# Handing over between stages of a decoder layer: when low weights, sums and the first input tile are made

## The chip, the cores and the metric

The kernel runs on one core of one Trainium2 chip. The metric is the time of one execution in device microseconds (us). Of the kernel before, three runs were timed: 2383.11, 2387.39 and 2387.43, median 2387.39.

## The reference: what is computed

One inference step of a decoder layer, for 256 tokens of a prompt and 8 single tokens of running requests (264 together), of width 2048, in float32:

```python
h = h + 0.5 * rmsnorm(swiglu(rmsnorm(h, ffn1_pre), ...), ffn1_post)     # FFN1
h = h + rmsnorm(mix(rmsnorm(h, mix_pre)), mix_post)                     # mixer
h = h + 0.5 * rmsnorm(swiglu(rmsnorm(h, ffn2_pre), ...), ffn2_post)     # FFN2
gate = sigmoid(rmsnorm(h, ple_pre) @ w_ple_gate)
h = h + rmsnorm(gate * (p @ w_ple_proj), ple_post)                      # PLE
```

`rmsnorm(x, g)` is `x * rsqrt(mean(x*x) + 1e-6) * g`, the mean over the 2048 channels of a token. `swiglu` is `(silu(x @ wg) * (x @ wu)) @ wd` with an inner width of 5632. `mix` projects its input, runs a gated convolution and a state-space scan (48 heads) side by side, and projects both back (the out-projection). The outputs are the layer's result and the new states of the convolutions and the scan.

## The kernel before

**Tiles.** Activations lie feature-major: a tile is 128 channels by 264 tokens, so a 2048-channel tensor is 16 tiles (KD = 16). `H(k)` is tile k of h, four to a buffer. A product with a weight matrix goes column by column: a column is 128 outputs, the sum over all k tiles of 128 x 128 weights in one bank of PSUM.

**Three matmuls for one.** Each float32 is split into a high part rounded for TensorE and a low part, the rest. `mm3` issues high weight by high input (L277), high weight by low input (L278) and low weight by high input (L279). For inputs `split` lets ScalarE write the high half (L268, `act<-h,vec`) and VectorE the low half (L244, `act<-h,vec,act`). For weights `Weights.load` brings a unit of 14 or 16 tiles by DMA from SyncE in two pieces of up to eight (L170), casts each to its high part on ScalarE (L172, `whi`) and subtracts on VectorE (L175, `wlo`). Of the buffers `wraw`, `whi` and `wlo` there are four each, and units are loaded two ahead of the one in use, so a cast starts when TensorE has read the last tile of an older piece.

**Stages.** FFN1, mixer, FFN2 and PLE follow each other with no gap but their norms. FFN1, FFN2 and PLE begin with a first pass (`gemm_first`): seven columns at a time over k = 0 to 15, unit by unit with two k tiles each, seven accumulators (two of them in the small banks `ps`). Then the rest goes column by column (`gemm_one`), for the FFNs in three chunks of the inner width with a down projection behind each (`ys`). The out-projection makes its columns in pairs (`gemm_pair`).

**Norms.** `SumSq.add` squares a tile on ScalarE and adds it to a running tile `run` (on GpSimd, for a first pass on VectorE); the last `direct` squares stay apart. `total` (L339) multiplies the parts by a matrix of ones, which sums over the channels and leaves the result on all partitions; one such matmul in float32 is two records of TensorE. `rsqrt` is a logarithm and an exponential on ScalarE. A first pass doesn't wait for its own norm, as the input isn't scaled by it: the scale is applied to the columns behind it. There `late` issues the total behind k tile 14 (of 0 to 15) as the scheduler finds room, and `eq` (L421, on VectorE) is made from it, a term that keeps the epsilon of the norm; the bank of the total is reused by the eighth column, which therefore waits until `eq` is read from it.

**A handover** is what lies between a stage's last column and the next stage's first matmul: the last addition to y (L241), its square (L268), the total, the scale `rs` (L268 twice), for the first tile the residual (`tmp<-y,vec,rr` at L244 and the addition to h at L241), its high and low halves, then the first matmul. TensorE does warm matmuls meanwhile (`warm`, L379), `HANDOVER = (4, 11)` of them ahead of the last part of the total and behind it; each is two records. `update_input` issues the handover's residuals and splits for tiles 0 to 3 in program order, the others as the scheduler places them.

**The order.** A scheduler with a model of the engines' times fixes one queue for each engine ahead of the run, and each engine works off its queue in that order. `high_priority`, `issue_after` and `keep_in_program_order` steer it.

**The tail.** `esq.total` gives the last norm. Then y = h + e*r is made tile by tile: on GpSimd for tiles 12 to 15, on VectorE by multiply and add, or, for the tiles in `TAIL_TENSOR`, by VectorE's multiply, two matmuls with the identity into PSUM (L1188 for h, L1220 for e) and a copy by ScalarE (L1221). Each finished tile or pair of tiles is stored (`store`, L1206).

## Time and profile before

| | us |
|---|---|
| median of three runs | 2387.39 |
| lowest and highest run | 2383.11, 2387.43 |
| the profiled execution's own time | 2383.33 |
| its span, first to last instruction | 2381.6 |
| mean granted clock of TensorE (1 is full speed) | 0.999 |
| low weights on VectorE (L175), busy | 978.1 |
| casts of weights on ScalarE (L172), busy | 831.4 |

The two last rows are from the page's groups, 814 instructions each. In a row of the timeline stand the start, the length, the engine, the line, the operation, the output and inputs, and in brackets how long the engine was idle before it and what ended that. Lengths of instructions that follow each other overlap a little; the distance of their starts is what one costs. For TensorE the ends are modelled, so distances of starts are used throughout. Names are shortened: `act` is a split input, `tmp` a temporary, `rr` a tile with a scale, `acc` and `ps` are banks of PSUM.

### The profile page before, as it was taken

How to read it: one execution, taken by the hardware profiler on the slowest of the kernel's cores; microseconds unless marked ns; L12 is line 12 of the kernel's file. 1: busy time of each engine (PE TensorE's matmuls, PEld its weight loads, DVE VectorE, ACT ScalarE, POOL GpSimd, SP SyncE). 2: the span in 40 equal slices, each digit the busy share in tenths (PEclk: the TensorE clock that was granted, in tenths of full speed). 3: DMA queues.
4: the chain of work that ended last, by engine and by line, in shares of the span. 5: the costliest groups of instructions: out<-in, count | busy, mean ns of one | idle time of the engine just before them, and what ended most of it. 6: DMA issues, size and time to landing. Idle time of an engine off the chain costs nothing.

```text
span 2381.6 us, 47454 instructions
## 1 busy us (share of the span) xinstructions
PE 2361.7 (99%) x19534; PEld 2342.3 (98%) x19534; DVE 1576.5 (66%) x2382; ACT 1186.8 (50%) x1787; POOL 178.0 (7%) x201
## 2 busy tenths in 40 slices
...
GB/s 260 217 184 182 184 184 182 185 184 182 184 173 183 257 229 230 215 222 211 224 214 180 180 168 236 163 232 244 227 211 228 238 241 212 221 234 207 179 206 134
DMA packets 163434, 489.89 MB, mean 206 GB/s; under 512 B 25312, under 2 KB 43024, under 8 KB 163216
## 3 DMA queue, kind: packets, MB, share of 16 engines
...
q14 instruction: 65, 0.53, 0.1%
...
## 4 chain that ended last, share of the span: by engine, by line
PE 94%; DVE 2%; ACT 2%; issue 1%; DMA 1%; SPq 0%; POOL 0%; ACTq 0%; DVEq 0%; POOLq 0%
PE acc L277 30%; PE acc L278 30%; PE acc L279 30%; PE ps L277 1%; PE ps L278 1%; PE ps L279 1%; DVE wlo L175 1%; ACT whi L172 1%; PE ps L339 1%; PE ps L906 1%; DMA wraw<-in_w 0%; PE ps L891 0%; DVE h L241 0%; DMA d_bc<-rows 0%; DVE ych L851 0%
## 5 line engine op out<-in xcount | busy, mean ns | idle before, releaser
L279 PE MATMUL acc<-act,wlo 128*128 128x264 f32 x6128 | 1733.0, 285 | 1.9 <-DVE wlo L175 1.9
L278 PE MATMUL acc<-act,whi 128*128 128x264 f32 x6128 | 1719.9, 282 | 0.0
L277 PE MATMUL acc<-act,whi 128*128 128x264 f32 x6128 | 1703.7, 282 | 2.5 <-ACT whi L172 2.2
L175 DVE TENSOR_TENSOR wlo<-wraw,whi 128x1024 fp32r<-128x1024 f32 (+2 forms) x814 | 978.1, 1204 | 584.9 <-ACT whi L172 581.3
L172 ACT CAST whi<-wraw 128x1024 fp32r<-128x1024 f32 (+2 forms) x814 | 831.4, 1024 | 974.2 <-PE acc L278 682.8
L277 PEld LDWEIGHTS acc<-act,whi 128*128 128x128 f32 x6128 | 1147.5, 189 | 5.1 <-ACT whi L172 2.9
L279 PEld LDWEIGHTS acc<-act,wlo 128*128 128x128 f32 x6128 | 1144.7, 187 | 5.5 <-DVE wlo L175 3.5
L278 PEld LDWEIGHTS acc<-act,whi 128*128 128x128 f32 x6128 | 1146.8, 187 | 1.9 <-issue 0.9
L241 POOL TENSOR_TENSOR run<-run,tmp 128x264 f32<-128x264 f32 x77 | 72.2, 938 | 889.6 <-ACT tmp L268 889.2
L244 DVE SCALAR_TENSOR_TENSOR y<-v,vec,y 128x245 f32<-128x245 f32 (+23 forms) x240 | 106.2, 465 | 0.6
L241 POOL TENSOR_TENSOR s<-s,eap 128x1024 f32<-128x1024 f32 x24 | 47.0, 1960 | 629.6 <-DMA s<-in_hst 534.4
L244 DVE SCALAR_TENSOR_TENSOR s<-bb,xds,s 128x128 f32<-128x128 f32 x192 | 52.7, 346 | 60.0 <-POOL s L241 60.0
L241 DVE TENSOR_TENSOR tmp<-acc,rr 128x264 f32<-128x264 f32 x99 | 42.5, 430 | 50.2 <-PE acc L279 50.2
L286 ACT CAST act<-tmp 128x264 fp32r<-128x264 f32 x104 | 41.9, 411 | 55.6 <-DVE tmp L241 50.9
L241 DVE TENSOR_TENSOR tmp<-tmp,acc 128x264 f32<-128x264 f32 x84 | 35.9, 428 | 39.9 <-PE acc L279 39.4
L241 DVE TENSOR_TENSOR act<-tmp,act 128x264 fp32r<-128x264 f32 x120 | 52.4, 441 | 0.5 <-ACT act L286 0.5
L278 PE MATMUL ps<-act,whi 128*128 128x264 f32 x192 | 52.3, 283 | 0.0
L279 PE MATMUL ps<-act,wlo 128*128 128x264 f32 x192 | 52.1, 284 | 0.0
L268 ACT ACTIVATE tmp<-tmp 128x264 f32<-128x264 f32 x112 | 47.0, 420 | 6.9 <-DVE tmp L241 6.7
L268 ACT ACTIVATE tmp<-y 128x264 f32<-128x264 f32 x67 | 28.0, 425 | 44.7 <-DVE y L241 43.3
L241 POOL TENSOR_TENSOR run<-run,y 128x264 f32<-128x264 f32 x7 | 7.2, 1029 | 576.7 <-ACT run L321 499.2
L241 DVE TENSOR_TENSOR y<-y,acc 128x264 f32<-128x264 f32 x80 | 34.0, 425 | 23.8 <-PE acc L279 23.8
(170 smaller groups left out, 1038.9 us busy)
## 6 DMA issues: line engine op xcount, KB each, us to landing
...
```

Of the source, the lines that this page charges most:

```text
L172: self.hi = nc.scalar.copy(hi[:, c:d], raw[:, c:d]).ins
L175: nc.vector.tensor_tensor(out=lo[:, c:d], in0=raw[:, c:d], in1=hi[:, c:d].bitcast(F32), op=ALU.subtract)
L241: return (eng or nc.vector).tensor_tensor(out=out, in0=in0, in1=in1, op=op)
L244: return nc.vector.scalar_tensor_tensor(out=out, in0=in0, scalar=scalar, in1=in1, op0=op0, op1=op1)
L268: i = nc.scalar.activation(out=out, in_=in_, func=func, bias=bias, scale=scale)
L277: nc.tensor.matmul(acc, hi, x[:, 0, :], start=first, stop=False)
L278: nc.tensor.matmul(acc, hi, x[:, 1, :], start=False, stop=False)
L279: traced[0] = nc.tensor.matmul(acc, lo, x[:, 0, :], start=False, stop=last).ins
L286: nc.scalar.copy(t[:, 0, :], x)
L339: m = nc.tensor.matmul(p, ones, s, start=i == 0, stop=last)
L906: nc.tensor.matmul(pd[64 * q : 64 * q + 64, P * c : P * c + P], xdt[c][:, 2 * j + q, :], ab[c][:, 2 * j + q, :], start=True, stop=True,)
```

## The change

1. *Low weights later at the two handovers.* For the unit loaded at the last pair of the out-projection, and for the one at the last down column of FFN2, `Weights.load(defer="second")` leaves both subtractions and the second cast for later. `flush` issues the first subtraction behind the last addition to y, the second cast and subtraction behind the last square.
2. *First input tile direct.* `update_input` no longer waits for the residual in h for tile 0. With the product of both gains (`both`, made once on GpSimd) VectorE forms t = y0 * both * rs, writes H(0) * pre + t once rounded, as the high half, and once in full, and subtracts for the low half. H(0)'s residual follows behind tile 3's. All squares of the new input go into `run`, so its total is one matmul and not two.
3. *The total in first passes.* `late` is now issued ahead of the fourth column of the last k tile, 12 matmuls before the end of the pass, and kept in program order.
4. *`eq` into the run.* In FFN2 `eq` is added to the run of squares by GpSimd ahead of the last chunk's end, so FFN2's total has two matmuls and not three.
5. *Tail.* Two of the tail's identity matmuls stand between the parts of the last total; the gain of the last e is applied on ScalarE behind the last exponential; seven tiles are summed by TensorE and not five, and these are stored by pairs: four single stores and six pairs in place of six and five.

Lines move by up to 54: L175 is L186 in the new code, L241 L264, L244 L267, L268 L291, L277 to L279 L300 to L302, L339 L364, L379 L404, L421 L446. The diff, cut to its core:

```diff
@@ -29,6 +29,7 @@
 HPG = 6
+GAINS = (("mix_post", "ffn2_pre"), ("ffn2_post", "ple_pre"))
 NH = 48
@@ -168,23 +171,43 @@
                     self.dma = nc.sync.dma_start(raw[:, c:d], src[:, a + c : a + d, :])
-                    with nullcontext() if behind is None else tc.issue_after(behind):
-                        self.hi = nc.scalar.copy(hi[:, c:d], raw[:, c:d]).ins
+                    def high(hi=hi[:, c:d], raw=raw[:, c:d]):
+                        self.hi = nc.scalar.copy(hi, raw).ins
+                    if a and defer == "second":
+                        self.later.append(high)
+                    else:
+                        with nullcontext() if behind is None else tc.issue_after(behind):
+                            high()
+                    def low(lo=lo[:, c:d], raw=raw[:, c:d], hi=hi[:, c:d]):
+                        self.lo = keep(
+                            nc.vector.tensor_tensor(out=lo, in0=raw, in1=hi.bitcast(F32), op=ALU.subtract)
+                        ).ins
+                    if defer:
+                        self.later.append(low)
+                        continue
                     with nullcontext() if self.hold is None else tc.issue_after(self.hold):
-                        self.lo = keep(
-                            nc.vector.tensor_tensor(
-                                out=lo[:, c:d], in0=raw[:, c:d], in1=hi[:, c:d].bitcast(F32), op=ALU.subtract
-                            )
-                        ).ins
+                        low()
                 if a // 8 < len(then):
...
         self.done.append(tiles)
-    def next(self, fill=True):
+    def flush(self, behind=None):
+        with self.tc.issue_after(behind) if behind else nullcontext(), self.tc.high_priority(offset=1000):
+            self.later.popleft()()
+    def next(self, fill=True, defer=None, more=False):
         want = min(self.at + 1 + self.AHEAD, len(PLAN))
         while fill and len(self.done) < want:
-            self.load()
+            self.load(defer=defer)
+        if more:
+            self.load(defer="second")
         tiles, self.done[self.at] = self.done[self.at], None
@@ -336,7 +359,9 @@
                         warm(idle[0], d)
-                    m = nc.tensor.matmul(p, ones, s, start=i == 0, stop=last)
+                    if last and between:
+                        between()
+                    m = keep(nc.tensor.matmul(p, ones, s, start=i == 0, stop=last))
             if idle[1]:
@@ -389,32 +414,32 @@
             for kk in range(per):
+                end = late and n == len(kts) - 1
                 for m in range(nm):
-                    i = mm3(accs[m], w[nm * kk + m], xs[kts[n]], n == 0, n == len(kts) - 1)
+                    if end and m == 3:
+                        late()
+                    keep = tc.keep_in_program_order if end and m else lambda ins: ins
+                    mm3(accs[m], w[nm * kk + m], xs[kts[n]], n == 0, n == len(kts) - 1, keep)
                 n += 1
-                if late and n == len(kts) - 2:
-                    late(i)
         return accs
-    def gemm_one(xs, kts, nunits=1, acc=None):
+    def gemm_one(xs, kts, acc=None, **how):
         acc = acc_tile() if acc is None else acc
-        n = 0
-        for _ in range(nunits):
-            for wt in ws.next():
-                mm3(acc, wt, xs[kts[n]], n == 0, n == len(kts) - 1)
-                n += 1
-        assert n == len(kts)
+        for n, wt in enumerate(ws.next(**how)):
+            mm3(acc, wt, xs[kts[n]], n == 0, n == len(kts) - 1)
+        assert n == len(kts) - 1
         return acc
-    def ffn(xs, sq, done):
+    def ffn(xs, sq, done, ysq, how):
         r, eq = rtile(), rtile()
         spare = []
-        def scale(behind):
-            p = sq.total(behind)
+        def scale():
+            p = sq.total(keep=tc.keep_in_program_order)
             spare.append(p)
@@ -447,8 +472,9 @@
                     bg.popleft()()
+            end = c == len(FF_CHUNKS) - 1
             for m in range(KD):
-                acc = gemm_one(mids, list(range(lo, hi)))
+                acc = gemm_one(mids, list(range(lo, hi)), **(how.get(m, {}) if end else {}))
                 if bg and m % 8 == 4:
@@ -456,9 +482,15 @@
                     with tc.high_priority() if m == KD - 1 else nullcontext():
-                        tt(ys[m], ys[m], acc, ALU.add)
-                if c == len(FF_CHUNKS) - 1:
+                        i = tt(ys[m], ys[m], acc, ALU.add)
+                if end:
+                    if ws.later:
+                        ws.flush(i.ins)
                     done(m, ys[m])
+                    while ws.later:
+                        ws.flush(ysq.squared)
+                    if m == 2 and ysq.n > KD:
+                        ysq.add_plain(eq)
             for f in range(lo, hi):
@@ -466,7 +498,8 @@
     def ffn_scale(ysq, eq, idle=(0, 0)):
-        ysq.parts.insert(0, eq)
+        if idle[0] == 0:
+            ysq.parts.insert(0, eq)
         rs = rtile()
@@ -494,6 +527,9 @@
     nc.sync.dma_start(vec[:, KD:], a["vec"][:, KD:])
+    both = cpool.tile([P, 2], F32, name="both")
+    for i, (post, pre) in enumerate(GAINS):
+        tt(both[:, i : i + 1], V(post), V(pre), ALU.mult, nc.gpsimd)
     sq = SumSq(KD, eng=nc.vector)
@@ -1077,26 +1113,37 @@
     for m in range(0, KD, 2):
-        accs = gemm_pair(list(range(CM)))
+        accs = gemm_pair(list(range(CM)), defer="second" if m == KD - 2 else None)
         if m < 8:
...
             with tc.high_priority() if m + i == KD - 1 else nullcontext():
-                tt(ys[m + i], ys[m + i], accs[i], ALU.add)
+                added = tt(ys[m + i], ys[m + i], accs[i], ALU.add)
             ysq.add(ys[m + i])
...
             table(LN_EXP)
-    def update_input(rs, post, pre):
-        xs, sq = [], SumSq(KD, eng=nc.vector)
+    ws.flush(added.ins)
+    while ws.later:
+        ws.flush(ysq.squared)
+    def update_input(rs, stage):
+        post, pre = GAINS[stage]
+        xs, sq = [], SumSq(KD, eng=nc.vector, direct=0)
         with tc.high_priority():
-            for k in range(5):
-                if k < 4:
-                    residual(k, ys[k], rs, post, tc.keep_in_program_order)
-                if k:
-                    xs.append(split(H(k - 1), V(pre, k - 1), tc.keep_in_program_order))
+            t, x, u = tmp(), act_tile(), tmp()
+            keep_order(stt(t, ys[0], both[:, stage : stage + 1], rs, ALU.mult, ALU.mult))
+            keep_order(stt(x[:, 0, :], H(0), V(pre), t, ALU.mult, ALU.add))
+            keep_order(stt(u, H(0), V(pre), t, ALU.mult, ALU.add))
+            keep_order(tt(x[:, 1, :], u, x[:, 0, :].bitcast(F32), ALU.subtract))
+            xs.append(x)
+            for k in range(1, 5):
+                residual(k % 4, ys[k % 4], rs, post, keep_order)
+                if k > 1:
+                    xs.append(split(H(k - 1), V(pre, k - 1), keep_order))
         for k in range(4, KD + 2):
@@ -1135,26 +1182,26 @@
         bg.append(lambda j=j: update_all(j))
-    ysq = SumSq(KD, urgent=True)
+    ysq = SumSq(KD + 1, urgent=True)
     def done2(m, y):
...
             table(LN_EXP)
-    ys, eq = ffn(xs, sq, done2)
+    ys, eq = ffn(xs, sq, done2, ysq, {KD - 1: dict(defer="second")})
     assert not bg
...
     rs = ffn_scale(ysq, eq, HANDOVER)
-    xs, sq = update_input(rs, "ffn2_post", "ple_pre")
+    xs, sq = update_input(rs, 1)
     r = rtile()
...
     spare = []
-    def scale(behind):
-        spare.append(sq.total(behind))
+    def scale():
+        spare.append(sq.total(keep=keep_order))
         rsqrt(r, spare[0], eps1, 1.0 / DM)
@@ -1172,12 +1219,12 @@
         esq.add(e)
-        act(e, e, AF.Identity, scale=V("ple_post", m))
+        if m < KD - 1:
+            act(e, e, AF.Identity, scale=V("ple_post", m))
     actx.close()
     tps = ctx.enter_context(tc.tile_pool(name="tps", bufs=1, space=PS))
-    total = esq.total()
     sums = []
@@ -1188,13 +1235,20 @@
             sums.append(p)
-    for _ in range(3):
-        begin_sum()
+    def begin_sums():
+        for _ in range(2):
+            begin_sum()
+    total = esq.total(keep=keep_order, between=begin_sums)
+    begin_sums()
     rp = ps_tile([P, T])
...
     act(rp, rs, AF.Exp, scale=-0.5)
-    act(rs, rs, AF.Exp, scale=-0.5)
+    last = act(rs, rs, AF.Exp, scale=-0.5).ins
+    e = e4[-1][:, 3, :]
+    with tc.issue_after(last):
+        act(e, e, AF.Identity, scale=V("ple_post", KD - 1))
     def pair(t, k, n):
@@ -1219,8 +1273,8 @@
                 nc.scalar.copy(H(i), p)
-                store(i, 1)
                 begin_sum()
+            store(k, n)
             continue
@@ -1229,8 +1283,8 @@
-TAIL_VECTOR = [(0, 2), (2, 1), (3, 1), (4, 2), (6, 2), (8, 2), (10, 2)]
-TAIL_TENSOR = [0, 1, 2, 4, 5]
+TAIL_VECTOR = [(0, 2), (2, 1), (3, 1), (4, 2), (6, 2), (8, 2), (10, 1), (11, 1)]
+TAIL_TENSOR = [0, 1, 2, 4, 5, 6, 7]
 TAIL_GENERAL = [(12, 2), (14, 2)]
```

Three places show how the scheduled order moves; the numbers at names tell buffers apart and differ a little between the two programs.

The first place is VectorE at the end of the mixer. `y_1002` and `y_1003` are the last two columns of the out-projection, `wlo_0` and `wlo_8` the two pieces of a unit's low weights, `rr` the scale. Before:

```order
L241 TENSOR_TENSOR y_1002_17821<-y_1002_17821,acc_18323 128x264
L175 TENSOR_TENSOR wlo_0_18327<-wraw_0_18325,whi_0_18326 128x1024
L241 TENSOR_TENSOR y_1003_17823<-y_1003_17823,acc_18324 128x264
L175 TENSOR_TENSOR wlo_8_18333<-wraw_8_18331,whi_8_18332 128x768
L244 SCALAR_TENSOR_TENSOR tmp_18414<-y_16521,vec,rr_18411 128x264
```

The same place in the new order:

```order
L264 TENSOR_TENSOR y_1002_17824<-y_1002_17824,acc_18326 128x264
L264 TENSOR_TENSOR y_1003_17826<-y_1003_17826,acc_18327 128x264
L186 TENSOR_TENSOR wlo_0_18330<-wraw_0_18328,whi_0_18329 128x1024
L186 TENSOR_TENSOR wlo_8_18335<-wraw_8_18333,whi_8_18334 128x768
L267 SCALAR_TENSOR_TENSOR tmp_18417<-y_16524,both,rr_18414 128x264
L267 SCALAR_TENSOR_TENSOR act_18418<-h_17890,vec,tmp_18417 128x264
L267 SCALAR_TENSOR_TENSOR tmp_18419<-h_17890,vec,tmp_18417 128x264
L264 TENSOR_TENSOR act_18418<-tmp_18419,act_18418 128x264
```

Both additions now stand ahead of both low weights, and the first input tile (`act_18418`) is written by VectorE alone.

The second place is VectorE in the first pass of FFN2, around the low half of the sixth input tile: `act_18455` before, `act_18462` in the new program. Before:

```order
L244 SCALAR_TENSOR_TENSOR act_18441<-h_17959,vec,act_18441 128x264
L175 TENSOR_TENSOR wlo_8_18577<-wraw_8_18575,whi_8_18576 128x768
L241 TENSOR_TENSOR run_18444<-run_18444,tmp_18458 128x264
L244 SCALAR_TENSOR_TENSOR tmp_18479<-y_970_17163,vec,rr_18411 128x264
L244 SCALAR_TENSOR_TENSOR act_18455<-h_17959,vec,act_18455 128x264
```

In the new order (`act_18448` is the fifth tile):

```order
L267 SCALAR_TENSOR_TENSOR act_18448<-h_17962,vec,act_18448 128x264
L264 TENSOR_TENSOR h_17962<-h_17962,tmp_18459 128x264
L264 TENSOR_TENSOR h_17962<-h_17962,tmp_18468 128x264
L186 TENSOR_TENSOR wlo_0_18633<-wraw_0_18631,whi_0_18632 128x1024
L264 TENSOR_TENSOR run_18451<-run_18451,tmp_18465 128x264
L264 TENSOR_TENSOR h_17962<-h_17962,tmp_18477 128x264
L186 TENSOR_TENSOR wlo_8_18639<-wraw_8_18637,whi_8_18638 128x768
L267 SCALAR_TENSOR_TENSOR tmp_18486<-y_970_17166,vec,rr_18414 128x264
L267 SCALAR_TENSOR_TENSOR act_18462<-h_17962,vec,act_18462 128x264
```

The unit `18633` and `18639` (`18625` and `18631` before, where both stand behind the sixth low half) is now ahead of it.

The third place is VectorE at the end of FFN1's first pass. Before:

```order
L175 TENSOR_TENSOR wlo_0_577<-wraw_0_575,whi_0_576 128x1024
L175 TENSOR_TENSOR wlo_8_583<-wraw_8_581,whi_8_582 128x1024
L421 TENSOR_SCALAR rr_315<-ps_629 128x264
L241 TENSOR_TENSOR tmp_690<-acc_316,rr_314 128x264
L175 TENSOR_TENSOR wlo_0_638<-wraw_0_636,whi_0_637 128x1024
```

In the new order:

```order
L186 TENSOR_TENSOR wlo_0_580<-wraw_0_578,whi_0_579 128x1024
L186 TENSOR_TENSOR wlo_8_586<-wraw_8_584,whi_8_585 128x1024
L186 TENSOR_TENSOR wlo_0_634<-wraw_0_632,whi_0_633 128x1024
L446 TENSOR_SCALAR rr_318<-ps_674 128x264
L264 TENSOR_TENSOR tmp_693<-acc_319,rr_317 128x264
```

`eq`, the instruction that reads the total's bank, stands behind one more low weight.

23 lines of the change are left out of this document (12 added, 11 removed).

## The prediction

> **What bounds the kernel now.** I read the page's shares first, then the waits of TensorE (PE), then the timeline of each engine at the places that the change touches.
>
> ```profile
> PE 2361.7 (99%) x19534; PEld 2342.3 (98%) x19534; DVE 1576.5 (66%) x2382; ACT 1186.8 (50%) x1787; POOL 178.0 (7%) x201
> ```
>
> PE is busy 99% of the span, so nothing that shortens another engine's work counts by itself. Only three things do: matmuls that go away, waits of PE that go away, and the tail, where PE has ended. The waits of PE in the stages that the change touches (us in total, times, longest):
>
> ```profile
> PE ps L339 <- DVE tmp L241: 1.5, 1, 1.5
> PE ps L339 <- ACT tmp L268: 0.8, 2, 0.4
> PE ps L277 <- DVE rr L421: 0.4, 1, 0.4
> ```
>
> The 1.5 is in the tail, the last 0.4 at the end of FFN2's first pass, and the 0.8 is twice 0.4, once in each handover. The view hides most of a handover, since PE does warm matmuls (L379) there, which do no work for the result. PE at the first one, from the mixer to FFN2:
>
> ```profile
> 1501.02 0.61 PE L339 MATMUL ps<-run,ones 128*128 128x264 f32 x2
> 1501.46 1.05 PE L379 MATMUL ps<-ident,ones 128*128 128x128 f32 x8
> 1502.91 0.71 PE L339 MATMUL ps<-tmp,ones 128*128 128x264 f32 x2 [0.40 <-ACT tmp L268]
> 1503.46 2.62 PE L379 MATMUL ps<-ident,ones 128*128 128x128 f32 x22
> 1506.27 0.88 PE L277 MATMUL acc<-act,whi 128*128 128x264 f32 x5 [0.19 <-ACT act L268]
> ```
>
> Call 1501.02, where the weights' matmuls are through, T0. The first matmul of FFN2 starts at T0+5.25: 1.89 to the last part of the sum of squares (L339 on `tmp`) and 3.36 from there. VectorE (DVE) in the same stretch:
>
> ```profile
> 1498.33 0.43 DVE L241 TENSOR_TENSOR y<-y,acc 128x264 f32<-128x264 f32 x1 [0.88 <-PE acc L279]
> 1500.78 1.23 DVE L175 TENSOR_TENSOR wlo<-wraw,whi 128x1024 fp32r<-128x1024 f32 x1 [2.02 <-ACT whi L172]
> 1501.92 0.42 DVE L241 TENSOR_TENSOR y<-y,acc 128x264 f32<-128x264 f32 x1
> ...
> 1504.71 0.49 DVE L244 SCALAR_TENSOR_TENSOR tmp<-y,vec,rr 128x264 f32<-128x264 f32 x1 [1.50 <-ACT rr L268]
> 1505.24 0.43 DVE L241 TENSOR_TENSOR h<-h,tmp 128x264 f32<-128x264 f32 x1
> ```
>
> And ScalarE (ACT):
>
> ```profile
> 1502.43 0.42 ACT L268 ACTIVATE tmp<-y 128x264 f32<-128x264 f32 x1 [0.47 <-DVE y L241]
> 1503.66 0.48 ACT L268 ACTIVATE rr<-ps,eps 128x264 f32<-128x264 f32 x1 [0.80 <-PE ps L339]
> 1504.17 0.42 ACT L268 ACTIVATE rr<-rr 128x264 f32<-128x264 f32 x1
> 1505.70 0.52 ACT L268 ACTIVATE act<-h,vec 128x264 fp32r<-128x264 f32 x1 [1.11 <-DVE h L241]
> ```
>
> The last addition (1501.92) stands behind a low weight (1500.78), and DVE was at it 1.14 us. Unobstructed, the addition follows its last matmul quickly: the one at 1498.33 starts 0.32 after this row.
>
> ```profile
> 1498.01 0.28 PE L279 MATMUL acc<-act,wlo 128*128 128x264 f32 x1
> ```
>
> **The change, part by part: handovers.** PE's last matmul here starts 0.12 ahead of T0 (its issue distance), so with the low weight out of the way the addition starts at about T0+0.20 in place of T0+0.90, which is 0.70 earlier. Square and total keep their distances (0.51 and 0.48), and the total could start at T0+1.19. But the four warm matmuls stand ahead of it on PE: eight records of about 0.116 (22 took 2.62, their last one's length included) from 1501.46 end at T0+1.37. So the deferral is worth 1.89 − 1.37 = **0.53** (rounded from the rows), not 0.70.
>
> Direct tile: in before one DVE pair (stt, addition) and ACT's high half come after the scale, in the new one DVE writes the high half by its second stt. One step of 0.49 goes (addition to high half: 1505.24 to 1505.70, and the matmul 0.57 after that, while a DVE result is taken some 0.1 sooner). But the eleven warm matmuls behind the total end 0.44 + 2.62 = 3.06 after its start, and the first weight matmul stands in PE's queue behind them: at 3.08 to 3.17, against 3.36. So only **0.19 to 0.28** of it is had. FFN2 starts 0.72 to 0.81 earlier, I take 0.75.
>
> This gain is spent again at the sixth input tile. In before DVE makes its low half by 1516.67:
>
> ```profile
> 1511.54 1.22 DVE L175 TENSOR_TENSOR wlo<-wraw,whi 128x1024 fp32r<-128x1024 f32 x1
> 1512.67 0.43 DVE L241 TENSOR_TENSOR run<-run,tmp 128x264 f32<-128x264 f32 x1
> ...
> 1514.58 0.95 DVE L175 TENSOR_TENSOR wlo<-wraw,whi 128x768 fp32r<-128x768 f32 x1
> 1515.44 0.42 DVE L241 TENSOR_TENSOR run<-run,tmp 128x264 f32<-128x264 f32 x1
> 1515.79 0.48 DVE L244 SCALAR_TENSOR_TENSOR tmp<-y,vec,rr 128x264 f32<-128x264 f32 x1
> 1516.19 0.48 DVE L244 SCALAR_TENSOR_TENSOR act<-h,vec,act 128x264 fp32r<-128x264 f32 x1
> ```
>
> and PE, in no hurry, takes it at
>
> ```profile
> 1519.71 0.28 PE L278 MATMUL acc<-act,whi 128*128 128x264 f32 x1
> ```
>
> From these rows DVE issues an stt every 0.40, an addition every 0.35, a low weight of 1024 columns every 1.13 and of 768 every 0.86; an instruction that needs the one before takes 0.13 more (1504.71 to 1505.24). Before, the queue from the first stt to this low half is 1516.67 − 1504.71 = 11.96. These stand there by the order: 15 stt, 10 additions, one low weight of each size, 6.0 + 3.5 + 1.13 + 0.86 = 11.5, and 0.47 for dependent pairs and the last one's own length. In the new order 17 stt, 12 additions or subtractions and two low weights of each size stand from the first stt to the sixth low half, both included: 6.8 + 4.2 + 4.0 = 15.0, with the same 0.47 and some three dependent pairs more (0.35) 15.8. The extra 3.8 are a second pair of low weights (2.0), which only the seventh and eighth tiles need and which before stood behind this low half, two stt and two additions (1.5), and those pairs. DVE starts at total + 1.80 = T0+3.17 and ends at T0+19.0; PE follows 0.1 to 0.2 later, at T0+19.15. PE wants it at T0+18.69 − 0.75 = T0+17.94. It therefore stalls 1.2 us, and after the sixth tile is later than before by 19.15 − 18.69 = **+0.46**. Bounds: no stall and −0.75 if the scheduler's two low weights found idle places, as in rival 1; +1.0 if the unplaced 0.8 comes to 1.3.
>
> [...]
>
> Second handover: the same additions and the same edits, and its total has the same wait of 0.40.
>
> ```profile
> 2270.72 0.71 PE L339 MATMUL ps<-tmp,ones 128*128 128x264 f32 x2 [0.40 <-ACT tmp L268]
> ```
>
> I count it the same, **+0.46**.
>
> Matmuls that go: each new input's sum of squares is one matmul in place of two, 0.44 each (1501.02 to 1501.46 is one): **−0.44** in FFN2 and **−0.44** in PLE. `eq` is added by POOL, so FFN2's end has one fewer, **−0.44**; POOL was busy 7% and has the time of 13 columns for it. That is this one:
>
> ```profile
> 1561.28 0.61 PE L339 MATMUL ps<-rr,ones 128*128 128x264 f32 x2
> ```
>
> **Placement of the total in first passes.** FFN2's is so late before that PE stops for the eighth column's bank:
>
> ```profile
> 1547.49 0.28 PE L279 MATMUL ps<-act,wlo 128*128 128x264 f32 x1
> 1548.20 0.39 PE L277 MATMUL ps<-act,whi 128*128 128x264 f32 x1 [0.42 <-DVE rr L421]
> ```
>
> That is 0.71 between starts where 0.12 is usual: 0.59 lost. The new place is 12 matmuls (1.44) ahead of the end, but `eq` (L446, L421 before) now stands behind a low weight on DVE, which leaves some 0.2: **−0.4** (0 to −0.6). PLE, whose total also stood late, **−0.1** (0 to −0.2, the slack of its smaller stop).
>
> FFN1's total moves the other way, from 36 matmuls before the end to 12, and one more low weight is put ahead of `eq`. PE wants the bank that `eq` frees here:
>
> ```profile
> 49.47 0.28 PE L277 MATMUL ps<-act,whi 128*128 128x264 f32 x1
> ```
>
> That low weight's cast waits until PE has done with a buffer, as this one does in before, 0.32 after this matmul's start:
>
> ```profile
> 49.23 0.28 PE L278 MATMUL ps<-act,whi 128*128 128x264 f32 x1
> ```
>
> ```profile
> 49.55 1.05 ACT L172 CAST whi<-wraw 128x1024 fp32r<-128x1024 f32 x1 [0.55 <-PE ps L278]
> ```
>
> By the order the extra one's buffer is free from the L278 at 47.07, which comes 0.88 sooner since the two matmuls of the total now come behind it: 46.2. Cast 46.5 to 47.55, low weight 47.6 to 48.8 (1.23), `eq` to 49.25: 0.2 of slack. **0** (0 to +0.3; rival 2).
>
> **Tail.** PE's last sums there stand within stores that saturate the DMA engines at the end, and DVE's shorter list (one tile pair fewer) is hidden by them. Only the packets count: four single tiles and six pairs in place of six and five. In a microsecond of single tiles, and in one of pairs alone (packets, MB, share of 16 engines):
>
> ```profile
> q1 hardware_dynamic: 283, 0.27, 79.6%
> ```
> ```profile
> q1 hardware_dynamic: 206, 0.40, 104.1%
> ```
>
> A single tile's packet takes 16 × 0.796 / 283 = 45 ns, a pair's, twice as big, 81. Two singles made a pair save 128 × (90 − 81) ns over 16 engines = 0.07 us, and by the rates 0.27 and 0.40 MB per us 0.3. I take **−0.2** (0 to −0.3). The move of the last gain on ACT behind the last exponential costs nothing, since PE's last part of the total, not ACT, sets the exponentials.
>
> The sum: FFN1 0; first handover +0.46 − 0.44 − 0.4 = −0.38; `eq` −0.44; second handover +0.46 − 0.44 − 0.1 = −0.08; tail −0.2. That is **−1.1 us**. The profiled execution took 2383.33 (its span is 2381.6, and 1.7 lie around it), so it would become 2382.2. The runs shown are 2383.11, 2387.39 and 2387.43: the profiled one lies with the lowest, and the median 4.1 above it. From the median the forecast is **2386.3**. Less than 0.2% of it (4.8 us) a measurement of this kernel can't tell from no change, as those runs lie 4.3 apart among themselves.
>
> **Rivals.** *1, DVE keeps up.* If the sixth tile's low half is there by T0+17.9 (the dependent pairs overlap, or PE's start is later than I think), both stalls of 1.2 vanish: −1.1 − 2.3 = −3.4, 2384.0 from the median. For it: before, this low half lay 3.0 ahead of PE, so DVE had air. Against: the queue is counted by rows, and it grew by 3.8. 15%.
>
> *2, FFN1's first pass (slower).* If the cast for the extra low weight comes later by more than the 0.2 of slack, PE waits for `eq` at 49.47. It pays up to a whole cast and low weight, 1.05 + 1.23 = 2.3, when the cast is queued behind another cast: −1.1 + 2.3 = +1.2, 2388.6. It decides over the sign from a delay of 1.3 upwards. For it: the slack is thin, and ACT has a table load between its casts nearby. Against: the new total lies later, so ACT isn't held by it when that buffer comes free. 9%.
>
> *3, the clock.* A stall that drops TensorE's clock costs more than itself. The start shows the price of a cold PE:
>
> ```profile
> 1.56 5.29 PE L379 MATMUL ps<-ident,ones 128*128 128x128 f32 x24 [1.56 <-POOL ident masks.py:199]
> ```
>
> 24 records took 5.29 where 22 took 2.62 later, 2.43 more. Were each of the two stalls of 1.2 to bring one such stretch, −1.1 + 4.9 = +3.8: 2391.2. Against: the wait of 1.5 for `tmp` in the waits above, longer than these, is followed by matmuls at full rate. 4%. [...]
>
> **How the numbers follow.** Forecast 72%, rivals 15, 9 and 4%. The likeliest time is 2386.3. The low end, 2381.0, is the lower of the two levels of the runs (2383.1) less 2.1, midway between my sum and rival 1; the high end is rival 2's 2388.6. Faster by over 0.2%: a quarter of the forecast's 72 (a result on the lower level), a third of rival 1: 24. Slower: a third of rival 3, an eighth of rival 2, a twentieth of the forecast: 6. The rest, 70, is within.
>
> **What would show it right or wrong.** Right: first matmul of FFN2 at T0+4.45 to 4.55, a PE wait at the sixth tile's L301 of about 1.2 (an `act` of DVE as its releaser) in both handovers, two sum matmuls fewer after them, no wait for `rr` at the eighth column in FFN1, and a tail with the last data some 0.2 sooner. Wrong: no such wait (rival 1), an `rr` wait in FFN1 of over 1 (rival 2), warm or weight matmuls at twice their 0.12 after a handover (rival 3), or a start at T0+5.2, by which the low weights weren't out of the way.

## The result: slower by 0.19%, and the profile after

The changed kernel took 2391.89 us (median of 14 runs, 2389.05 to 2396.38), the kernel before in as many runs 2387.62 (2383.11 to 2392.49). The ratio is 1.0019, 95% interval 1.0011 to 1.0028: a loss of 4.3 us by the medians, where 1.1 us of gain was forecast. The profiled execution took 2390.26 with a span of 2388.5, against 2383.33 and 2381.6.

The page's shares of the changed kernel:

```profile
PE 2369.0 (99%) x19536; PEld 2349.2 (98%) x19536; DVE 1580.7 (66%) x2391; ACT 1188.7 (50%) x1787; POOL 180.9 (8%) x204
```

PE is busy 7.3 us longer than before (2361.7), with the same weight matmuls. A loss by waiting would have left PE's busy time alone; this one is inside it. The waits of PE show what the change did as planned:

```profile
PE acc L301 <- DVE act L267: 1.8, 2, 0.9
...
PE sum L1274 <- DVE e L264: 1.3, 1, 1.3
PE ps L364 <- DVE tmp L264: 0.3, 1, 0.3
```

The wait for `rr` is gone, as are both for ACT's square (`tmp L268`); the stall at the sixth tile is there in both handovers. In the tail PE waits 0.3 us for `tmp` and 1.3 for `e`, where it waited 1.5 and 0.4 before (`PE sum L1220 <- DVE e L241: 0.4, 1, 0.4`). PE at the first handover:

```profile
1508.07 0.61 PE L364 MATMUL ps<-run,ones 128*128 128x264 f32 x2
1508.51 1.05 PE L404 MATMUL ps<-ident,ones 128*128 128x128 f32 x8
1509.40 0.61 PE L364 MATMUL ps<-tmp,ones 128*128 128x264 f32 x2
1509.85 2.62 PE L404 MATMUL ps<-ident,ones 128*128 128x128 f32 x22
1512.22 0.85 PE L300 MATMUL acc<-act,whi 128*128 128x264 f32 x5
...
1525.62 0.41 PE L300 MATMUL ps<-act,whi 128*128 128x264 f32 x2
1526.88 0.39 PE L301 MATMUL acc<-act,whi 128*128 128x264 f32 x1 [0.85 <-DVE act L267]
```

T0 is 1508.07 here. The total's last part comes at T0+1.33 (1.89 before), the first matmul at T0+4.15 (5.25 before), the sixth tile's first low matmul at T0+18.81 (18.69 before). VectorE (DVE) in the same stretch:

```profile
1508.27 0.43 DVE L264 TENSOR_TENSOR y<-y,acc 128x264 f32<-128x264 f32 x1 [2.45 <-PE acc L302]
1508.61 2.31 DVE L186 TENSOR_TENSOR wlo<-wraw,whi 128x1024 fp32r<-128x1024 f32 x2
1511.10 0.49 DVE L267 SCALAR_TENSOR_TENSOR tmp<-y,both,rr 128x264 f32<-128x264 f32 x1 [0.17 <-ACT rr L291]
...
1525.06 0.95 DVE L186 TENSOR_TENSOR wlo<-wraw,whi 128x768 fp32r<-128x768 f32 x1
1525.93 0.49 DVE L267 SCALAR_TENSOR_TENSOR tmp<-y,vec,rr 128x264 f32<-128x264 f32 x1
1526.34 0.89 DVE L267 SCALAR_TENSOR_TENSOR act<-h,vec,act 128x264 fp32r<-128x264 f32 x2
```

The addition starts at T0+0.20 ahead of both low weights. The sixth low half, the first of the last row's two, ends near 1526.8: 15.7 us of queue.

**Where the 7 us are.** One window of FFN1, long after its first pass and away from every edit, in the kernel before (columns: PE, its weight loads, DVE, ACT, POOL busy with counts; the granted clock; DMA share; GB/s):

```profile
100.00:700.00 600.00, 600.00 (x5002) 600.00 (x5002) 305.88 (x333) 246.64 (x298) 8.89 (x17) 1.00 0.58 182
```

The same window of the changed kernel:

```profile
100.00:700.00 600.00, 600.00 (x4957) 600.00 (x4956) 303.60 (x330) 243.12 (x294) 7.03 (x14) 1.00 0.56 181
```

PE is busy without a gap in both, the granted clock is 1.00 in both, and in 600 us the changed kernel does 45 matmuls fewer. The mean distance from start to start is 120.00 ns before and 121.11 after. The whole stretch behind the first pass, from the start of its last matmul to the mixer's first, takes 720.6 and 727.1 us. The slower pace begins at one instruction, FFN1's matmul of `eq`:

```profile
60.28 0.28 PE L300 MATMUL acc<-act,whi 128*128 128x264 f32 x1
60.40 0.61 PE L364 MATMUL ps<-rr,ones 128*128 128x264 f32 x2
60.65 0.48 PE L301 MATMUL acc<-act,whi 128*128 128x264 f32 x1
60.97 0.29 PE L302 MATMUL acc<-act,wlo 128*128 128x264 f32 x1
```

Ahead of it the mean distance is 120.0, behind it 121.1, for all 710 us that FFN1 still has. So the experiments ask two things: are the handovers worth what was forecast, and what sets the pace.

### The profile page after: what moved, and what is told of

The parts are those of the page before. It is cut to its first block, busy times and chain, and to the rows that moved or that the text cites. A ratio compares the mean times of both kernels' runs of the same rounds, so it can differ in the third digit from the quotient of the medians.

```text
span 2388.5 us, 47460 instructions
## 1 busy us (share of the span) xinstructions
PE 2369.0 (99%) x19536; PEld 2349.2 (98%) x19536; DVE 1580.7 (66%) x2391; ACT 1188.7 (50%) x1787; POOL 180.9 (8%) x204
## 3 DMA queue, kind: packets, MB, share of 16 engines
q10 hardware_dynamic: 2080, 1.04, 0.2%
## 4 chain that ended last, share of the span: by engine, by line
PE 93%; DVE 3%; DMA 2%; ACT 1%; issue 1%; SPq 0%; ACTq 0%; POOL 0%; DVEq 0%; POOLq 0%
PE acc L302 29%; PE acc L301 29%; PE acc L300 29%; DVE wlo L186 1%; PE ps L300 1%; PE ps L301 1%; PE ps L302 1%; DMA wraw<-in_w 1%; PE ps L364 1%; ACT whi L176 1%; PE ps L942 0%; DMA d_bc<-rows 0%; DVE h L264 0%; PE ps L927 0%; PE ps L404 0%
## 5 line engine op out<-in xcount | busy, mean ns | idle before, releaser
L302 PE MATMUL acc<-act,wlo 128*128 128x264 f32 x6128 | 1737.9, 285 | 1.6 <-DVE wlo L186 1.5
L300 PE MATMUL acc<-act,whi 128*128 128x264 f32 x6128 | 1705.7, 282 | 3.9 <-ACT whi L176 3.9
L186 DVE TENSOR_TENSOR wlo<-wraw,whi 128x1024 fp32r<-128x1024 f32 (+2 forms) x814 | 977.7, 1203 | 584.4 <-ACT whi L176 581.3
L302 PEld LDWEIGHTS acc<-act,wlo 128*128 128x128 f32 x6128 | 1148.6, 188 | 5.1 <-DVE wlo L186 3.0
L300 PEld LDWEIGHTS acc<-act,whi 128*128 128x128 f32 x6128 | 1146.8, 189 | 6.4 <-ACT whi L176 4.9
L264 POOL TENSOR_TENSOR run<-run,tmp 128x264 f32<-128x264 f32 x77 | 71.9, 933 | 896.6 <-ACT tmp L291 896.2
L267 DVE SCALAR_TENSOR_TENSOR y<-v,vec,y 128x245 f32<-128x245 f32 (+23 forms) x240 | 105.8, 463 | 0.6
L264 POOL TENSOR_TENSOR s<-s,eap 128x1024 f32<-128x1024 f32 x24 | 48.3, 2014 | 628.3 <-DMA s<-in_hst 575.8
L267 DVE SCALAR_TENSOR_TENSOR s<-bb,xds,s 128x128 f32<-128x128 f32 x192 | 52.5, 345 | 55.4 <-POOL s L264 55.4
L264 DVE TENSOR_TENSOR tmp<-acc,rr 128x264 f32<-128x264 f32 x99 | 42.5, 430 | 52.7 <-PE acc L302 52.6
L264 DVE TENSOR_TENSOR tmp<-tmp,acc 128x264 f32<-128x264 f32 x84 | 35.9, 427 | 40.6 <-PE acc L302 40.6
L264 DVE TENSOR_TENSOR act<-tmp,act 128x264 fp32r<-128x264 f32 x122 | 54.8, 454 | 0.2
L264 DVE TENSOR_TENSOR y<-y,acc 128x264 f32<-128x264 f32 x80 | 34.0, 425 | 29.6 <-PE acc L302 29.5
L302 PE MATMUL ps<-act,wlo 128*128 128x264 f32 x192 | 52.2, 284 | 0.0
L264 POOL TENSOR_TENSOR run<-run,y 128x264 f32<-128x264 f32 x7 | 7.2, 1031 | 578.1 <-ACT run L344 500.6
L291 ACT ACTIVATE tmp<-y 128x264 f32<-128x264 f32 x67 | 28.0, 425 | 45.4 <-DVE y L264 44.0
L291 ACT ACTIVATE tmp<-tmp 128x264 f32<-128x264 f32 x112 | 46.9, 420 | 7.1 <-DVE tmp L264 6.9
```

What stands on the lines that cost most here:

```text
L186: nc.vector.tensor_tensor(out=lo, in0=raw, in1=hi.bitcast(F32), op=ALU.subtract)
L264: return (eng or nc.vector).tensor_tensor(out=out, in0=in0, in1=in1, op=op)
L267: return nc.vector.scalar_tensor_tensor(out=out, in0=in0, scalar=scalar, in1=in1, op0=op0, op1=op1)
L291: i = nc.scalar.activation(out=out, in_=in_, func=func, bias=bias, scale=scale)
L300: keep(nc.tensor.matmul(acc, hi, x[:, 0, :], start=first, stop=False))
L302: traced[0] = keep(nc.tensor.matmul(acc, lo, x[:, 0, :], start=False, stop=last)).ins
```

## The experiments

Eighteen experiments ran, each 10 to 12 times (one_more_warm 4, pool_sixth_tail 5). The times go against runs of the kernel before on the same chip. The table has the ratio with its interval and, from each profile, that same stretch of FFN1 behind its first pass (us).

| kernel | median | ratio (95%) | FFN1 |
|---|---|---|---|
| after_again | 2390.93 | 1.0016 (1.0007 to 1.0024) | 727.1 |
| before_again | 2386.28 | 0.9993 (0.9983 to 1.0002) | 720.6 |
| eq_in_run | 2390.15 | 1.0013 (1.0004 to 1.0021) | 720.1 |
| sixth_first | 2391.82 | 1.0019 (1.0010 to 1.0028) | 727.1 |
| eq_between | 2385.12 | 0.9996 (0.9987 to 1.0004) | 720.6 |
| eq_early | 2386.08 | 0.9997 (0.9989 to 1.0006) | 720.6 |
| before_eq_late | 2387.03 | 1.0002 (0.9993 to 1.0011) | 720.6 |
| old_tail | 2387.14 | 0.9998 (0.9990 to 1.0007) | 720.6 |
| pool_sixth_tail | 2395.36 | 1.0034 (1.0021 to 1.0047) | 720.6 |
| one_more_warm | 2397.23 | 1.0049 (1.0034 to 1.0065) | 727.1 |
| fewer_warm | 2383.02 | 0.9987 (0.9978 to 0.9996) | 720.6 |
| old_total_ffn1 | 2391.80 | 1.0025 (1.0016 to 1.0033) | 727.2 |
| after_pad | 2391.70 | 1.0023 (1.0014 to 1.0032) | 727.1 |
| before_late_pad | 2391.04 | 1.0018 (1.0010 to 1.0027) | 727.1 |
| before_pad | 2391.35 | 1.0020 (1.0012 to 1.0029) | 727.2 |
| no_shift | 2387.64 | 1.0008 (0.9999 to 1.0018) | 720.6 |
| no_shift_best | 2385.75 | 0.9997 (0.9987 to 1.0007) | 720.6 |
| before_pad128 | 2386.02 | 1.0003 (0.9994 to 1.0011) | 720.6 |

**Is the pace drawn or set?** The two kernels once more, without an edit.

> The changed kernel as it is, once more. Theory A (pace): its loss isn't in waits but in the pace of TensorE's matmuls, which in a stretch start every 120.0 or every 121.1 ns, and something drawn anew in each execution at each interruption of the stream decides between them. Then its profile shows other stretches at 121.1 ns than the first one's (63 to 775, 1557 to 1706), and its span can come anywhere from 2381 to 2390. Theory B (the program decides): the same two stretches at 121.1 ns again, a span of 2387 to 2390, and a time of some 2390 to 2393 beside 2386 to 2389 of the kernel before. Theory C (the forecast's stalls): two waits of TensorE for the sixth input tile, 0.9 us each, in every execution; they are 1.8 us together and can't give 4.3.

> The kernel before as it is, timed against itself. It shows what a measurement can tell: a ratio of 1.000 with an interval of about 0.1%. Theory A: its profile shows stretches at 121.1 ns at other places than the first one's (1283 to 1402 alone), some 0.9 us of span for each 100 us at the slower pace. Theory B: the same single stretch again, span 2381 to 2383.

FFN1 came out at 727.1 and 720.6 again. Set by the program, then, not drawn (theory A falls). That holds for FFN1 alone. In a part of FFN2 the pace did differ between two executions of the same kernel: over the 1427 matmuls from its eighth column on the changed kernel took 172.75 us once and 171.41 once. The spread of the times lies mostly in the mixer, 731 to 737 us in these four profiles.

**Is it eq's matmul?** eq_in_run takes it away.

```diff
-    ysq, hy, yy = (SumSq(KD, f"run{i}", ep, urgent=not i) for i in range(3))
+    ysq, hy, yy = (SumSq(KD + (not i), f"run{i}", ep, urgent=not i) for i in range(3))
...
-        if idle[0] == 0:
-            ysq.parts.insert(0, eq)
```

> The changed kernel with the term eq of FFN1 added to the run of squares as well, as the change does in FFN2: the one float32 matmul that stands between a column's matmuls some 13 us after FFN1's first pass goes away. By the forecast's prices it is worth 0.44 us. Theory A or B, both with the switch at that matmul (in the changed kernel the pace went from 120.0 to 121.1 just there, at 60.4): FFN1 stays at 120.0 from its first pass on, 710 us, and the time falls by 6.6 + 0.4 = 7.0 us against the changed kernel, to about 2385 to 2386, at or below the kernel before. Rival: the pace isn't set by the interruption but by what the engines read and write beside it; then FFN1 runs at 121.1 again and the time falls by 0.4.

FFN1 fell to 720.1, as the theory had it, but the time only to 2390.15: with this edit the scheduler reordered the mixer, which took 740.8 us. The time proves nothing here; the stretch does. The next edit moves nothing else but one pair of neighbours on ScalarE and VectorE.

Ahead of the tenth column's first triple, FFN1 now puts eq's matmul in program order:

```diff
+            if n == 0:
+                put()
+            K(nc.tensor.matmul(acc, hi, x[:, 0, :], start=n == 0, stop=False))
...
+            self.p = ps_tile([P, T])
+            tc.keep_in_program_order(nc.tensor.matmul(self.p, ones, eq, start=True, stop=False))
```

> The changed kernel with one instruction of TensorE moved by two places: FFN1's float32 matmul of eq, which stands behind the first matmul of the last triple of the ninth column, now stands behind that triple, between two columns. All else in the five queues is the same but for one pair of neighbours on ScalarE and VectorE beside it. Theory B (the program decides, and the place of an interruption in a triple is what counts): FFN1 runs at 120.0 ns and not 121.1 from there to its end, 710 us, the span and the time fall by 6.5 us, to about 2384 to 2385, some 2 to 3 below the kernel before. Theory A (drawn anew in each execution): one look can show either, the time by the median lies between. Rival, the placement has nothing to do with it: 121.1 again, no change in time.

Its rows at this place (helpers have new lines; L442, L445 and L446 are the three matmuls):

```profile
60.66 0.29 PE L302 MATMUL acc<-act,wlo 128*128 128x264 f32 x1
60.79 0.61 PE L355 MATMUL ps<-rr,ones 128*128 128x264 f32 x2
61.04 0.48 PE L442 MATMUL acc<-act,whi 128*128 128x264 f32 x1
```

and its window of FFN1:

```profile
100.00:700.00 600.00, 600.00 (x5003) 600.00 (x5002) 305.88 (x333) 246.72 (x297) 8.65 (x17) 1.00 0.57 182
```

One instruction of TensorE two places later, and FFN1 is 6.56 us shorter and the ratio 0.9996. The loss of the change is this pace. Two more kernels put it inside a triple with the same edit (`n == 7` and `n == 15` of the ninth column, behind the first matmul), to ask whether such a place is enough to cause it.

> The changed kernel with that same matmul put where the kernel before has it: one column's middle, behind the first matmul of the eighth triple of the ninth column, inside a triple still. If any place inside a triple gives 121.1, FFN1 stays slow and the time stays at 2391. If it is this one program's exact place (the kernel before ran at 120.0 with it here, twice), FFN1 runs at 120.0 and the time falls by 6.5 to 2384 to 2385.

The scheduler answered this edit by putting the first eight triples of the tenth column ahead, so eq's matmul came between the last matmul of a triple of one column and the second of a triple of the other, not where it was wanted. FFN1 ran at 120.0; the case says less than it was meant to.

> The kernel before with the same matmul put where the changed kernel has it: behind the first matmul of the last triple of the ninth column, eight triples later than it stood. Nothing else of the change is in it. Theory B by place: FFN1 goes to 121.1 ns there, and the time rises by 6.5 us, to 2393 to 2394, ratio 1.0027, more than the whole change cost. If the cause is something else in the changed kernel (the later total, the extra low weight on VectorE), FFN1 stays at 120.0 and the time stays at 2387.

720.6: the changed kernel's place does no harm in the kernel before. Place alone isn't the cause, and the theory of the place falls as stated.

**Which part of the change, then?** one_more_warm (`warm(13)`) shifts TensorE's stream by two records; old_total_ffn1 undoes the later total in FFN1 alone:

```diff
+                if soon and n == len(kts) - 2:
+                    late(i)
...
-        accs = gemm_first(xs, k16, 8, FIRST_FF, scale)
+        accs = gemm_first(xs, k16, 8, FIRST_FF, scale, soon=ysq.n == KD)
```

> The changed kernel with thirteen warm matmuls at its start in place of twelve; the order in FFN1 is the same, eq's matmul in the same place of the same triple, two records later in TensorE's stream (the mixer's order moves somewhat). If the pace behind eq's matmul hangs on where it stands in the triple and on what stands beside it, FFN1 runs at 121.1 ns again, 727 us in place of 720.5. If it hangs on the count of what TensorE has done before, or on a phase in time, it can come out at 120.0, and the time falls by 6.5.

> The changed kernel with one part undone, in FFN1's first pass alone: its total is again issued behind k tile 14, so that eq is ready sooner and eq's matmul falls back to the place of the kernel before, eight triples earlier. From there on the five queues are those of the changed kernel. Theory (this part of the change, by moving eq's matmul, set off the slower pace): FFN1 runs at 120.0 ns, 720.6 us from the eighth column to its end in place of 727.1, and the time falls by 6.5 us against the changed kernel, to about 2384 to 2386. Rival (another part of the change did, such as the shift of all tiles in SBUF): 121.1 ns and 2391.

Both at 121.1. A shift of the stream makes no difference (its time is longer for other reasons too: another order in the mixer, 737.5 us), and with eq's matmul back in the very place of the kernel before the pace stays slow. No placement that the change made is to blame. What is left is where the tiles lie: the new tile `both` takes 32 bytes of each partition, and all tiles allocated behind it (inputs, weights, scales) lie 32 bytes further. (The traces hold no addresses; the shifts are reckoned from the widths of the tiles and the steps of 32 bytes in which they are allocated.) Three kernels change addresses alone; no instruction moves in any queue:

```diff
-    both = cpool.tile([P, 2], F32, name="both")
+    both = cpool.tile([P, 10], F32, name="both")     # after_pad: 32 bytes more
```
```diff
-    eps1 = cpool.tile([P, 1], F32, name="eps1")
+    eps1 = cpool.tile([P, 9], F32, name="eps1")[:, :1]     # before_pad, before_late_pad: 32 bytes more
```

> The changed kernel with its tile of gain products ten columns wide in place of two. It takes 64 bytes of a partition in place of 32, so that all tiles allocated behind it lie 32 bytes further; no instruction moves. The tile of gain products was new with the change, and put all those tiles 32 bytes further than in the kernel before, where the same place of eq's matmul gave 120.0 ns. Theory (place and address together decide): with another 32 bytes FFN1 runs at 120.0 ns again, 720.6 us, and the time falls by 6.5 us, to about 2384 to 2386. Rival (addresses have no part): 727.1 us and 2391.

> before_eq_late (the kernel before with eq's matmul in the changed kernel's place) with a tile at the start widened so that the tiles behind it lie 32 bytes further, as in the changed kernel; no instruction moves. Theory (place and address together decide): FFN1 goes to 121.1 ns, 727.1 us, and the time rises by 6.5 us, to about 2393. Rival (addresses have no part): 120.0 ns, 720.6 us, and 2387.

> The kernel before with that same widened tile, eq's matmul in its own place; no instruction moves. Theory (place and address together decide, and the slow pair is the changed kernel's): FFN1 stays at 120.0 ns, 720.6 us, and the time at 2386 to 2388. If the address alone decides: 727.1 us and 2393.

The window of before_pad, which is the kernel before with 32 bytes more in one tile:

```profile
100.00:700.00 600.00, 600.00 (x4957) 600.00 (x4956) 303.26 (x330) 243.39 (x294) 10.37 (x22) 1.00 0.56 181
```

That is the whole loss of the change, ratio 1.0020, without one line of what the change does. before_late_pad came out as expected, the other two not: the old place of eq's matmul doesn't protect it, so "place and address together" was too narrow, and 64 bytes (after_pad) are as bad as 32.

**The change without the shift.** no_shift puts the two columns into the 32 bytes that the tile of epsilon holds anyway; before_pad128 shifts the kernel before by 128.

```diff
-    eps1 = cpool.tile([P, 1], F32, name="eps1")
+    eps = cpool.tile([P, 3], F32, name="eps1")
+    eps1 = eps[:, :1]
...
-    both = cpool.tile([P, 2], F32, name="both")
+    both = eps[:, 1:]
```

> The changed kernel with its two columns of gain products put into the unused part of the 32 bytes that the tile of epsilon has already, so that every tile lies where it lay in the kernel before; no instruction moves. Theory (the 32 bytes are the loss): FFN1 runs at 120.0 ns, 720.6 us from the eighth column on in place of 727.1, and the time falls by 6.5 us against the changed kernel, to about 2385, ratio to the kernel before 0.999 to 1.000; what is left is what the change's instructions do, by the stages of the profiles so far some 1 to 2 us less than the kernel before. Rival (the later place of eq's matmul is slow with these addresses too): 727.1 us and 2391.

> The kernel before with the tile at the start widened so that all tiles behind it lie 128 bytes further (32 in before_pad, which ran FFN1 at 121.1 ns); no instruction moves. If the address counts by its place in a period of 128 bytes, FFN1 runs at 120.0 ns, 720.6 us, and the time is that of the kernel before, 2387. If the kernel before merely lies at a lucky address: 121.1 ns, 727.1 us, and 2391 to 2393.

Their windows, no_shift first:

```profile
100.00:700.00 600.00, 600.00 (x5002) 600.00 (x5001) 305.79 (x333) 246.61 (x297) 7.47 (x16) 1.00 0.56 182
```
```profile
100.00:700.00 600.00, 600.00 (x5002) 600.00 (x5002) 305.45 (x333) 246.59 (x297) 8.19 (x16) 1.00 0.57 182
```

All instructions of the change, at the old addresses: 120.0 ns, span 2381.7, and no loss that can be told from none (1.0008, interval 0.9999 to 1.0018). The median of 2387.64 is 2 to 3 us above what I expected; the new tail, which varies by up to 2.7 us (below), and the mixer lie in it, and I can't part them. A shift by 128 is harmless for FFN1, and its span of 2380.5 is the shortest of all: with it a stretch of the mixer (from about 1300 on, 897 matmuls) also ran at 120.0, which was at 121.1 in each of the other nineteen profiles.

**Handovers.** In sixth_first the residuals of tiles 1 to 6 and the splits of 1 to 5 stand in program order, tile 0's residual behind them; pool_sixth_tail has that on top of old_tail, with the squares of the new input added up by GpSimd; fewer_warm has seven warm matmuls behind the total.

```diff
-            for k in range(1, 5):
-                residual(k % 4, ys[k % 4], rs, post, keep_order)
+            for k in range(1, 7):
+                residual(k, ys[k], rs, post, keep_order)
...
-        xs, sq = [], SumSq(KD, eng=nc.vector, direct=0)     # pool_sixth_tail
+        xs, sq = [], SumSq(KD, direct=0)
...
-HANDOVER = (4, 11)     # fewer_warm
+HANDOVER = (4, 7)
```

> The changed kernel with the residuals of tiles 1 to 6 and the splits of 1 to 5 kept in program order on VectorE, and tile 0's residual behind them, so that less stands ahead of the sixth tile's low half. Theory C: the two waits of 0.9 us for the sixth tile go, and the time falls by 1.8 us, if no later tile waits instead. Theories A and B: the waits go and the span falls by up to 1.8, but the difference to the kernel before remains, 2 to 4 us, with the slow stretches; by A they can lie elsewhere.

The sixth tile no longer stalls, a later one does:

```profile
1531.91 0.40 PE L300 MATMUL ps<-act,whi 128*128 128x264 f32 x2
1532.86 0.39 PE L301 MATMUL acc<-act,whi 128*128 128x264 f32 x1 [0.55 <-DVE act L267]
```

From FFN2's first matmul to its eighth column it took 13.77 + 28.52 = 42.3 us, with the matmul behind the sixth tile's first low one as divide; the changed kernel took 14.88 + 27.43 = 42.3. Reordering gains nothing: VectorE's queue is as long as before.

> old_tail, with the squares of both new inputs added up by GpSimd and not by VectorE, and the residuals of tiles 1 to 6 and splits of 1 to 5 in program order ahead of tile 0's residual. Theory (VectorE's queue is what stalls TensorE at the sixth tile, 1.1 us in each handover; in the kernel that only reordered it, the stall came back two tiles later as 0.8): with 15 additions of 0.35 less in VectorE's queue in each first pass both stalls go, 2 x 1.1 us, and the time falls by up to 2.2 against old_tail, to about 2382. Rival: GpSimd, 0.94 us for an addition, delivers the sum late, and TensorE waits for the total's bank at the eighth column instead.

```profile
PE acc L301 <- DVE act L267: 7.6, 2, 3.9
```

Less work for VectorE, and yet two waits of 3.9, and 13.77 + 34.13 = 47.9 us. The order isn't to blame: the same six low weights stand ahead of the eighth tile's low half in sixth_first and here. VectorE's instructions are longer. In pool_sixth_tail GpSimd adds from 1522.67 on without a break:

```profile
1522.67 8.57 POOL L264 TENSOR_TENSOR run<-run,tmp 128x264 f32<-128x264 f32 x8 [2.90 <-ACT tmp L291]
1524.56 1.99 DVE L267 SCALAR_TENSOR_TENSOR tmp<-y,vec,rr 128x264 f32<-128x264 f32 x2 [0.65 <-POOL run L264]
1527.88 0.96 DVE L264 TENSOR_TENSOR h<-h,tmp 128x264 f32<-128x264 f32 x1
1528.77 0.96 DVE L267 SCALAR_TENSOR_TENSOR act<-h,vec,act 128x264 fp32r<-128x264 f32 x1
```

The same pair of stt (SCALAR_TENSOR_TENSOR) took this in sixth_first:

```profile
1527.31 0.89 DVE L267 SCALAR_TENSOR_TENSOR tmp<-y,vec,rr 128x264 f32<-128x264 f32 x2
```

VectorE waits 0.65 us for an addition of GpSimd before it writes its next `tmp`, and beside GpSimd's additions it takes 0.96 us for what took 0.43 or 0.48 alone. Late in the stall TensorE's granted clock falls to 0.50 for 6.8 us, and its matmuls come 0.22 us apart:

```profile
1528.80:1535.60 6.80, 5.81 (x26) 5.81 (x27) 6.80 (x12) 4.62 (x10) 3.25 (x5) 0.50 0.19 59
```

26 matmuls at 0.22 in place of 0.12 are some 2.7 of the 5.6 us lost here (an estimate from this row), and PLE's first pass shows the same from 2300.2 on. So GpSimd's help cost VectorE more than it saved; neither the theory nor the stated rival, a late sum, is what happened.

> eq_between with seven warm matmuls behind the last part of the total at both handovers in place of eleven; nothing else moves in the five queues. The four take 0.9 us. Theory (VectorE sets when the sixth tile's low half is there): FFN2 and PLE start earlier by at most what the first tile allows, some 0.3 to 0.6, and the stall at the sixth tile grows by the same, so that the tile's first low matmul comes at the same time and the kernel's time doesn't move (less than 0.2). Rival (TensorE's own count sets it): each handover is 0.3 to 0.6 shorter, 0.6 to 1.2 together. Third case: TensorE idles long enough for its clock to fall, and the first matmuls behind run at twice their 0.12.

FFN2 started 0.04 us sooner and PLE 0.15, both were back at the same time behind the sixth tile (4.24 + 14.93 against 4.28 + 14.88): the start came forward by far less than the 0.3 to 0.6 expected, since with four warm matmuls fewer TensorE waits for the first tile (two waits of up to 0.6). The granted clock stayed at 1.00 in both handovers. Its ratio, 0.9987 (0.9978 to 0.9996), is the best of all and below both kernels; its stages are those of eq_between to 0.2 us but for the mixer (731.7 and 735.5), so I don't credit the four matmuls with it.

**Tail.** old_tail is eq_between with the tail of the kernel before; no_shift_best has the old addresses too.

> eq_between (the changed kernel with FFN1's eq matmul between two columns) with the tail of the kernel before: five tiles by TensorE, six single stores and five pairs, the last gain ahead of the logarithm, the total ahead of the identity matmuls. In the traces so far the tail, from the last weight matmul to the end, took 14.3 us in three profiles of the old form, and 14.4, 14.5, 14.5, 15.9, 16.1 and 16.2 in six of the new one, with 1.3 us between two stores where TensorE waits for e. Theory: the new tail costs 0.1 to 1.9 us, most often either; the old one brings 14.3 in every profile, and the time falls by 0 to 1.5, to some 2384. Rival (the forecast): the new tail is worth 0.2, and the time rises by that.

> no_shift with eq's matmul between two columns and with the tail of the kernel before. FFN1 at 120.0 ns, the tail 14.3 us in place of 14.4 to 17.1, the handovers as in the changed kernel: start of FFN2 and PLE 1.0 to 1.1 sooner, 1.1 to 1.2 of stall at the sixth tile each. Expected: 2384 to 2386, ratio 0.999, at or below both kernels. Where FFN1 comes out at 121.1: 2391.

From the last weight matmul to the end the old tail took 14.30 to 14.38 us in nine profiles, the new one 14.38 to 17.11 in eleven, 15.1 in the mean. Where the least of the loss comes from stands in the changed kernel's rows (its tail took 14.52). PE waits for `e`:

```profile
2378.74 1.60 PE L1274 MATMUL sum<-e,ident 128*128 128x264 f32 x6 [1.29 <-DVE e L264]
```

The stores go out one behind another on SyncE's queue (SP), and one store of a pair waits 0.8 us for ScalarE's copy of a tile, where in the kernel before no store behind the first waits over 0.3:

```profile
SPq L1260 <- ACT h L1275: 0.8, 1, 0.8
```

So the fifth store starts 1.28 us behind the fourth, where all starts lay 0.44 to 0.56 apart before, and the DMA engines, at 0.98 a moment before, stand at 0.62 for a microsecond, where those of the kernel before only rose, window by window, to 1.04:

```profile
2382.00:2383.00 1.00, 1.00 (x6) 0.87 (x5) 0.93 (x3) 0.47 (x2) 0.92 (x2) 1.00 0.98 374
2383.00:2384.00 1.00, 0.90 (x5) 0.42 (x3) 0.93 (x3) 0.44 (x2) 0.82 (x1) 1.00 0.62 234
2384.00:2385.00 1.00, 0.00 (x0) 0.00 (x0) 0.29 (x1) 0.32 (x1) 0.00 (x0) 1.00 1.02 376
```

The kernel before in its tail, for comparison:

```profile
2375.00:2376.00 1.00, 0.42 (x2) 0.00 (x1) 0.93 (x3) 0.76 (x2) 0.92 (x2) 1.00 0.88 314
2376.00:2377.00 1.00, 0.00 (x0) 0.00 (x0) 0.97 (x2) 0.00 (x0) 1.00 (x1) 1.00 0.98 341
2377.00:2378.00 1.00, 0.00 (x0) 0.00 (x0) 0.96 (x2) 0.00 (x0) 0.10 (x1) 1.00 1.02 362
```

That is worth 0.1 to 0.2 us, and seven of the eleven new tails lie there. The other four are 1.5 to 2.7 longer, and their traces differ. In old_total_ffn1 (17.11) and sixth_first (16.06) TensorE's granted clock is at 0.50 for 3.4 us behind the wait for `e`, and the same six records take 2.88 us in old_total_ffn1 in place of 1.60:

```profile
2379.97 2.88 PE L1276 MATMUL sum<-e,ident 128*128 128x264 f32 x6 [1.29 <-DVE e L264]
```
```profile
2380.20:2383.50 3.30, 3.30 (x8) 2.51 (x8) 3.23 (x7) 1.14 (x3) 3.22 (x3) 0.50 0.21 70
```

In eq_in_run (16.16) a store waits 1.8 us for GpSimd's `e`, and in after_again (15.93) the last store's data lands a microsecond later. How much of each loss these account for isn't worked out. In the nine old tails the clock stayed at 1.00 until TensorE was through.

## Why the prediction was wrong, step by step

The step that failed is the first: "Only three things do: matmuls that go away, waits of PE that go away, and the tail". There is a fourth, the distance at which PE's matmuls follow each other where nothing waits. I took 0.12 us for it, at every place and after the change as before, and put the new tile `both` at nothing without a reason: it stands in no term of the sum. Its 32 bytes cost 6.6 us in FFN1. Rival 3 had the shape, a stretch of matmuls that gets slower for a small cause, and the wrong mechanism: the granted clock stays at 1.00 in FFN1 (changed kernel, 50 to 770), and it did so at the change's own two stalls of 0.9 us. The clock does fall elsewhere: to 0.50 at the stalls of 3.9 us in pool_sixth_tail and in two of the new tails, and, in 15 of the 20 profiles, somewhere in the mixer (the clock's mean over the span is 0.996 to 1.000 in the 20).

The other steps, from stage times between the same matmuls of the profiles (us, changed less before):

| term | forecast | measured |
|---|---|---|
| FFN1's first pass, to the eighth column | 0 | none to be told: 48.7 to 49.6 in six profiles of the old form, 48.6 to 49.8 in eleven of the new one; 49.9 in old_total_ffn1, 50.2 in one_more_warm and 51.4 in after_pad, where the granted clock was at 0.50 for 3.4 us |
| FFN1's other columns (pace) | not in the sum | +6.56 |
| start of FFN2, of PLE | −0.75 each | −1.10, −1.00 |
| stall at the sixth tile | +1.2 each | +1.21, +1.14 |
| one sum matmul and the bank's wait, FFN2 | −0.84 | −0.82 |
| one sum matmul, PLE | −0.54 | −0.66 |
| `eq` into the run | −0.44 | −0.45 (+0.9 in the three profiles in which the pace was slow there too) |
| tail | −0.2 | +0.1 to +2.8, +0.8 in the mean |

Without pace and tail these come to −1.10 + 1.21 − 0.82 − 0.45 − 1.00 + 1.14 − 0.66 = −1.7; with the tail's mean −0.9, where −1.1 stood. That the two are so near is in part luck: each start came 0.25 to 0.35 sooner than forecast, and the tail lost that again. The five kernels with the new handovers, the old mixer order or nearly so and FFN1 at 120.0 agree with that: 0.9996, 0.9997, 0.9998, 0.9987 and 0.9997, with no_shift at 1.0008. But all of their intervals except fewer_warm's include 1, so the handovers' gain is read from the stages and not shown by the times.

- The stall at the sixth tile was right in mechanism and size: 15.7 us of queue where 15.8 was counted. sixth_first shows that it is the queue's load, fewer_warm that it, and not the start, sets the time. (The count takes it that no instruction of VectorE passes another, with 32 of them ahead of this low half. At the six places for which VectorE's queue is listed above, the traces of the two kernels have its instructions start in just that order, in the changed kernel from 1522.15 to this low half at 1526.34; beyond these places it is the author's assumption.)
- The start was undersized. I let the eleven warm matmuls end 0.44 + 2.62 after the total began; 2.62 is a group's length with its last record's own modelled length in it, and the first matmul followed 2.37 after the first warm one. The direct tile was ready by then.
- FFN1's wait for `eq` (rival 2) did not come: no wait for `rr` stands in the new waits. Rival 1 is refuted by the two waits of 0.9.
- The tail was wrong. I argued that VectorE's list was hidden behind the stores and priced packets alone. But with two more tiles by TensorE and pair stores that wait for both tiles, a store comes later and the DMA engines get a hole (0.1 to 0.2 us); in four profiles of eleven more was lost, by TensorE's clock, by a wait for GpSimd or by a late landing. Why these four executions and not the others isn't settled.
- Two slips in the sums change nothing: midway between −1.1 and rival 1's −3.4 is −2.25, not −2.1, so the low end would be 2380.9 and not 2381.0, and the shares named for a faster time add up to 23 and not 24.
